# A 90-degree rotation of an 8192 x 8192 array: two early stores cut into halves with 8 KB reads

## The chip, the cores and the metric

The kernel runs on one core of one Trainium2 chip. The metric is the device time in microseconds; a kernel's time is the median of its runs. A profile is one execution taken by the hardware profiler, whose span is about 2 us shorter than the time of the run.

## The reference, cut to what matters

```python
def setup_inputs():
    return {"x": np.random.randn(8192, 8192).astype(np.float32), "k": 1}

def reference(x, k):
    return np.rot90(x, k)
```

The array is 268 MB. It has to be read once and written once.

## The kernel before

The array is worked through in macro tiles of 1024 rows by 4096 columns. A macro tile comes in by eight loads of 128 rows (2 MB each, one 16 KB run for each partition). VectorE copies each load, with blocks of columns mirrored, into eight chunk buffers; TensorE (PE in the profile) transposes 128 x 128 blocks into PSUM; ScalarE copies PSUM to an output tile and issues the store. A macro tile has eight outputs, numbered by `i`; each is stored by one transfer of 2 MB. `S` is the number of 128-row groups that one store carries: with `S = G = 4` each partition gives one run of 16 KB, with `S = PW = 2` a run of 8 KB.

```python
a_pool = ...(name="a_pool", bufs=2)     # loads
r_pool = ...(name="r_pool", bufs=63)    # chunks, 64 to a macro tile
o_pool = ...(name="o_pool", bufs=3)     # outputs
# ...
            for j in range(W // CH):
                ar = r_pool.tile([P, CH // P, P], dt, tag="ar")
                nc.vector.tensor_copy(out=ar[:], in_=a[:, j * CH : (j + 1) * CH]...[:, :, ::-1])
                chunks[t, j] = ar
# ... in store():
        for i, g0 in enumerate(range(0, W // P, G)):
            # ...
            S = PW if end and r0 + rows == N and g0 + G == W // P else G
            # ...
            for h in range(0, G, PW):
                # ... transpositions into ps[h // PW]
                nc.scalar.copy(o[:, G - PW - h : G - h, :], ps[h // PW])
                done = h + PW
                if done % S == 0:
                    # ...
                    nc.scalar.dma_start(out=dst, in_=o[:, G - done : G - done + S, :])
```

Of the kernel before, what the change touches and what calls it, by code (L numbers as in the profile page):

```python
# [2 lines left out]

# [5 lines left out]

P = 128  # L10




R = 1024
RT = R // P
LAST = [4, 4]
W = 4096
CH = 512
F = 4096  # L20
FP = 2048


def whole_reads(nc):






    for fn in nc.m.functions:
        for block in fn.blocks:
            for n, ins in enumerate(block.instructions):
                if not isinstance(ins, mybir.InstDMACopy):
                    continue
                src = ins.ins[0]
                ap = [list(d) for d in src.ap]
                if len(ap) == 3 and ap[2][0] == 1 and ap[1][0] == ap[2][1]:
                    ap = [ap[0], [1, 1], [1, ap[1][1] * ap[2][1]]]
                    block.instructions[n] = copy.replace(  # L40
                        ins,
                        ins=[copy.replace(src, ap=ap)],
                        ant_dge_precooked=False,
                    )


def macro_tiles(N, M):

    tiles = [(r0, RT, c0) for r0 in range(0, N, R) for c0 in range(0, M, W)]
    r0, _, c0 = tiles.pop()  # L50
    for n in LAST:
        tiles.append((r0, n, c0))
        r0 += n * P
    return tiles


@with_exitstack
def kernel(
    ctx: ExitStack,
    tc: tile.TileContext,  # L60
    x: bass.AP,
    k: bass.AP,
    out: bass.AP,
):
    nc = tc.nc
    assert k == 1, f"only k=1 supported, got {k}"
    nc.at_finalize(whole_reads)

    N, M = x.shape
    dt = x.dtype  # L70

    consts = ctx.enter_context(tc.tile_pool(name="consts", bufs=1))
    ident = consts.tile([P, P], dt)
    make_identity(nc, ident)

    a_pool = ctx.enter_context(tc.tile_pool(name="a_pool", bufs=2))
    r_pool = ctx.enter_context(tc.tile_pool(name="r_pool", bufs=63))
    o_pool = ctx.enter_context(tc.tile_pool(name="o_pool", bufs=3))
    psum_pool = ctx.enter_context(
        tc.tile_pool(name="psum", bufs=2, space=bass.MemoryType.PSUM)  # L80
    )

    loads = 0

    def load(r0, rt, c0):





        nonlocal loads
        chunks = {}
        for t in range(rt):


            if loads < RT and loads % 5 >= 2:
                a = o_pool.tile([P, W], dt, tag="o")
            else:
                a = a_pool.tile([P, W], dt, tag="a")
            loads += 1  # L100
            nc.sync.dma_start(  # L101
                out=a[:], in_=x[r0 + t * P : r0 + (t + 1) * P, c0 : c0 + W]
            )
            for j in range(W // CH):
                ar = r_pool.tile([P, CH // P, P], dt, tag="ar")
                nc.vector.tensor_copy(  # L106
                    out=ar[:],
                    in_=a[:, j * CH : (j + 1) * CH].rearrange(
                        "r (b m) -> r b m", m=P
                    )[:, :, ::-1],  # L110
                )
                chunks[t, j] = ar
            yield chunks

    def store(r0, rt, c0, chunks, end):





        rows = rt * P
        PW = 1
        while 2 * PW * rows <= FP:
            PW *= 2
        G = PW
        while 2 * G * rows <= F:
            G *= 2
        for i, g0 in enumerate(range(0, W // P, G)):
            if end and i % 2:
                ot = a_pool.tile([P, F], dt, tag="a")  # L130
            else:
                ot = o_pool.tile([P, F], dt, tag="o")
            o = ot[:, : G * rows].rearrange("m (g f) -> m g f", g=G)

            S = PW if end and r0 + rows == N and g0 + G == W // P else G


            ps = {}

            def transposes(t, ws):  # L140
                for w in ws:
                    g = g0 + w
                    nc.tensor.transpose(  # L143
                        ps[w // PW][:, PW - 1 - w % PW, t * P : (t + 1) * P],
                        chunks[t, g * P // CH][:, g % (CH // P), :],
                        ident,
                    )

            def psum_tile(h):
                pt = psum_pool.tile([P, FP], mybir.dt.float32, tag="ps")  # L150
                ps[h] = pt[:, : PW * rows].rearrange("m (g f) -> m g f", g=PW)

            if i == 0 and (rt == RT or r0 + rows < N):
                for h in range(G // PW):
                    psum_tile(h)
                for t in range(rt):
                    transposes(t, range(G))
            for h in range(0, G, PW):
                if h // PW not in ps:
                    psum_tile(h // PW)  # L160
                    for w in range(h, h + PW):
                        for t in range(rt):
                            transposes(t, [w])
# [4 lines that stand above are left out]
                    top = M - c0 - (g0 + done) * P  # L168
                    dst = out[top : top + S * P, r0 : r0 + rows].rearrange(
                        "(g m) f -> m g f", g=S  # L170
                    )
                    nc.scalar.dma_start(  # L172
                        out=dst, in_=o[:, G - done : G - done + S, :]
                    )
            yield

    tiles = macro_tiles(N, M)
    *most, before_last, last = tiles
    for m in most:
        *_, chunks = load(*m)  # L180
        for _ in store(*m, chunks, False):
            pass


    *_, chunks = load(*before_last)
    outputs = store(*before_last, chunks, True)
    rows = load(*last)
    for _ in range(last[1] - 1):
        next(rows)
    next(outputs)  # L190
    chunks = next(rows)
    for _ in outputs:
        pass
    for _ in store(*last, chunks, True):
        pass


# [1 line left out]
_INS = ['x', 'k']  # L199
_OUTS = [((8192, 8192), 'float32')]  # L200

_NUMBERS = {'k': 1}


# [26 lines left out]
```

## Time and profile before

| | before |
|---|---|
| time, median (6 runs) | 1267.82 us |
| bytes moved | 537.55 MB |
| usual DMA rate | 429 GB/s |
| first and last engine at the last store | 1258.41 and 1264.90 us |

The prediction below shows the main lines of this profile. Three more of the page matter later. Two are the queues of kind "instruction" (records, MB, share of the 16 engines); the third is the chain that ended last, by line.

```profile
q8 instruction: 32, 0.52, 0.2%
q14 instruction: 17, 0.14, 0.0%
...
DMA a<-in_x_dram 48%; DMA out_dram<-ot 30%; ACT ot L164 8%; DVE ar L106 8%; PE pt L143 5%; ACTq L172 0%; DVEq L106 0%; ACTq L164 0%; SPq L101 0%
```

### The profile page before, as it was taken

The page shows a single profiled execution, that of the slowest core. Times are in us where ns is not written, and L with a number is a line of the kernel's source. Part 1 is how long each engine was busy: PE and PEld are TensorE (multiplying, and loading weights), DVE is VectorE, ACT ScalarE, POOL GpSimd, SP SyncE. Part 2 cuts the span into 40 slices and gives each one's busy share as a digit, 9 for nine tenths or more (in the row PEclk, how much of TensorE's full clock was granted, in tenths as well). Part 3 has the DMA queues.
Part 4 walks back from the last instruction along what each step waited for, and adds up shares of the span by engine and source line. Part 5 has one row for each costly group of instructions (what it writes and reads, how often), then busy time and mean ns, then how long its engine had stood idle before and what let it go on. Part 6 is the DMA issues. An engine that isn't in the chain of part 4 may idle for free.

```text
span 1265.8 us, 10385 instructions
## 1 busy us (share of the span) xinstructions
PE 685.3 (54%) x4096; PEld 639.3 (51%) x4096; DVE 355.3 (28%) x1024; ACT 467.8 (37%) x257; POOL 0.7 (0%) x6
## 2 busy tenths in 40 slices
PE   1555545555555554564555546566464655546573
PEld 1544444554445454554545545565454655545572
DVE  4423322232222322232222322233222332223210
ACT  0433334333343333433424334243442434324363
POOL 0000000000000000000000000000000000000000
PEclk9977877768777777777777776776767776767777
DMA  9999999999999999999999999999999999999998
GB/s 398 426 429 429 428 429 429 428 431 427 429 429 429 428 430 429 429 428 429 429 429 428 429 421 430 427 430 429 423 429 428 418 429 428 428 429 425 428 422 334
DMA packets 37057, 537.55 MB, mean 425 GB/s; under 512 B 4112, under 2 KB 4112, under 8 KB 4112
## 3 DMA queue, kind: packets, MB, share of 16 engines
q10 hardware_dynamic: 18576, 268.44, 50.0%
q1 hardware_dynamic: 18432, 268.44, 49.8%
q8 instruction: 32, 0.52, 0.2%
q14 instruction: 17, 0.14, 0.0%
HBM read 268.44 MB, written 268.44 MB: 424 GB/s over the span
## 4 chain that ended last, share of the span: by engine, by line
DMA 77%; ACT 8%; DVE 8%; PE 5%; issue 1%; ACTq 0%; DVEq 0%; SPq 0%
DMA a<-in_x_dram 48%; DMA out_dram<-ot 30%; ACT ot L164 8%; DVE ar L106 8%; PE pt L143 5%; ACTq L172 0%; DVEq L106 0%; ACTq L164 0%; SPq L101 0%
## 5 line engine op out<-in xcount | busy, mean ns | idle before, releaser
L143 PE MATMUL pt<-ident,ar 128*128 128x128 f32 x4096 | 685.3, 344 | 560.7 <-ACT ot L164 396.1
L143 PEld LDWEIGHTS pt<-ident,ar 128*128 128x128 f32 x4096 | 639.3, 183 | 606.5 <-ACT ot L164 433.2
L164 ACT COPY ot<-pt 128x2048 f32<-128x2048 f32 x256 | 466.5, 1869 | 755.5 <-DMA out_dram<-ot 506.3
L106 DVE COPY ar<-a 128x512 f32<-128x512 f32 x1024 | 355.3, 422 | 865.4 <-DMA a<-in_x_dram 827.9
L164 ACT ACT_TABLE_LOAD x1 | 1.3, 1283 | 25.6 <-DVE ar L106 25.6
masks.py:199 POOL TENSOR_SCALAR_AFFINE_SELECT ident<-ident 128x128 f32<-128x128 f32 x1 | 0.3, 292 | 0.1
masks.py:197 POOL MEMSET ident<- 128x128 f32 x1 | 0.2, 204 | 0.3 <-POOLq L212 0.3
L212 POOL MEMSET const-bfloat16-1.0<- 128x1 bf16 x1 | 0.1, 102 | 0.0
L212 POOL MEMSET const-uint8-127<- 128x1 uint8 x1 | 0.1, 102 | 0.0
L212 POOL MEMSET const-float32-0.0<- 128x1 f32 x1 | 0.1, 99 | 0.2 <-issue 0.2
L212 POOL MEMSET const-float32-1.0<- 128x1 f32 x1 | 0.1, 99 | 0.0
## 6 DMA issues: line engine op xcount, KB each, us to landing
a<-in_x_dram SPq DMA_DIRECT2D x128, 2048.0 KB, 16.7
out_dram<-ot ACTq DMA_DIRECT2D x127, 2048.0 KB, 25.6
out_dram<-ot ACTq DMA_DIRECT2D x2, 1024.0 KB, 14.9
```

The source lines that it names most:

```text
L106: nc.vector.tensor_copy(out=ar[:], in_=a[:, j * CH : (j + 1) * CH].rearrange("r (b m) -> r b m", m=P)[:, :, ::-1],)
L143: nc.tensor.transpose(ps[w // PW][:, PW - 1 - w % PW, t * P : (t + 1) * P], chunks[t, g * P // CH][:, g % (CH // P), :], ident,)
L164: nc.scalar.copy(o[:, G - PW - h : G - h, :], ps[h // PW])
L212: nc = _bacc.Bacc("TRN2", target_bir_lowering=False, num_devices=1)
```

## The change

In the first macro tile, the fifth and the seventh output are stored in two halves, each with 8 KB reads. The intent, as I read it from the name `lead`, is to let the loads get ahead of the stores for a while. A record, below, is one run of bytes that a DMA engine moves, as the profile lists it; the lead is the bytes loaded minus the bytes stored so far. The prediction works out how half-sized store records could raise the lead.

```diff
-            S = PW if end and r0 + rows == N and g0 + G == W // P else G
+            lead = r0 == 0 and c0 == 0 and i in (4, 6)
+            S = PW if lead or (end and r0 + rows == N and g0 + G == W // P) else G
```

## The prediction

> **What bounds the kernel now.** I read first the share of each engine and the DMA rows, then the chain that ended last, then the waits, then the DMA throughput in short windows, and last the landing times of single transfers.
>
> The page of the kernel before, its busy shares, DMA rows, queues and chain:
>
> ```profile
> span 1265.8 us, 10385 instructions
> PE 685.3 (54%) x4096; PEld 639.3 (51%) x4096; DVE 355.3 (28%) x1024; ACT 467.8 (37%) x257; POOL 0.7 (0%) x6
> ...
> DMA  9999999999999999999999999999999999999998
> GB/s 398 426 429 429 428 429 429 428 431 427 429 429 429 428 430 429 429 428 429 429 429 428 429 421 430 427 430 429 423 429 428 418 429 428 428 429 425 428 422 334
> ...
> q10 hardware_dynamic: 18576, 268.44, 50.0%
> q1 hardware_dynamic: 18432, 268.44, 49.8%
> ...
> DMA 77%; ACT 8%; DVE 8%; PE 5%; issue 1%; ACTq 0%; DVEq 0%; SPq 0%
> ```
>
> No compute engine is over 54%; the 16 DMA engines are over 90% in every slice but the last. Loads (q1) and stores (q10) move the same bytes and take the same time. Where the chain names ACT, DVE or PE, the DMA share is still 9, so those links cost nothing. The waits agree: VectorE and ScalarE wait for transfers, and VectorE for a free chunk (a PE release) only six times.
>
> ```profile
> DVE ar L106 <- DMA a<-in_x_dram: 827.9, 123, 10.1
> ACT ot L164 <- DMA out_dram<-ot: 506.3, 91, 7.1
> ...
> DVE ar L106 <- PE pt L143: 37.5, 6, 7.6
> ```
>
> The floor follows: 537.55 MB at the usual 429 GB/s is 1253 us. The other 12.8 us of the span I look for in windows (columns after the engines: granted clock, DMA share, GB/s):
>
> ```profile
> 0.00:10.00 10.00, 1.08 (x4) 0.71 (x4) 1.86 (x6) 0.00 (x0) 0.70 (x6) 1.00 0.84 334
> ...
> 750.00:760.00 10.00, 7.25 (x58) 6.72 (x56) 2.77 (x8) 5.03 (x4) 0.00 (x0) 0.93 1.01 408
> 905.00:915.00 10.00, 8.86 (x64) 8.35 (x64) 2.87 (x9) 5.80 (x4) 0.00 (x0) 0.83 1.00 408
> 980.00:990.00 10.00, 6.30 (x29) 5.91 (x30) 2.77 (x8) 5.11 (x3) 0.00 (x0) 0.50 1.01 415
> 990.00:1000.00 10.00, 7.72 (x54) 7.25 (x54) 2.77 (x8) 5.89 (x4) 0.00 (x0) 0.84 0.99 405
> ...
> 1250.00:1260.00 10.00, 0.00 (x0) 0.00 (x0) 0.00 (x0) 0.00 (x0) 0.00 (x0) 0.50 0.89 369
> ```
>
> Three losses show. The head loses (429 - 334)/429 x 10 = 2.2 us. Four windows at the start of a macro tile's stores fall below 429: (21 + 21 + 14 + 24)/429 x 10 = 1.9 us, as a mean over the engines. The tail is uneven: of the last store's sixteen landings the first is at 1258.41 and the last at 1264.90, with a mean lag of 1.7 us, so the slowest DMA engine ends 4.8 us after the average. That skew grew over the run: 0.5 us at the first load, 1.7 us at the load landing at 105 us, 9.6 us at the stores near 1200 us. The steps that widen it early fall beside the small instruction-queue transfers (q8 and q14). The end is therefore the total work of the slowest of sixteen engines, which is never idle.
>
> **What the Trainium skill says.** "DMA: Bandwidth & Descriptors", section "Where 436 GB/s comes from", puts the ceiling at 435.2 GB/s for a core; the trace's 429 is 98.6% of it, so there is no bandwidth to win. The same page's section "Queues, rings and completion order" says that each engine round-robins between the queue rows with work, switching at packet boundaries. The trace agrees with equal turns: with 16 KB records on both sides the two queues share the rate evenly (about 214 GB/s each when I sum the records in 10 us steps from 100 us on). The same page, section "Why small descriptors are slow (HBM only)", gives a fixed overhead of about 3 cycles per packet, worst at 256 bytes; by that, 8 KB is far from the small case. The trace agrees: in the pure-store tail an 8 KB record takes 315 ns and a 16 KB one 626 ns (medians).
>
> **The change part by part.** A store of a full macro tile is 2 MB, 128 partitions of one 16 KB read each. The timeline of ScalarE shows the issues of the first macro tile: the fifth at 73.74 and the seventh at 93.41.
>
> ```profile
> 70.08 3.63 ACT L164 COPY ot<-pt 128x2048 f32<-128x2048 f32 x2 [6.71 <-DMA out_dram<-ot]
> 73.74 0.55 ACTq L172 DMA_DIRECT2D out_dram<-ot  x1
> ...
> 89.74 3.63 ACT L164 COPY ot<-pt 128x2048 f32<-128x2048 f32 x2 [6.30 <-DMA out_dram<-ot]
> 93.41 0.55 ACTq L172 DMA_DIRECT2D out_dram<-ot  x1
> ```
>
> - Added: two DMA issues of 0.55 us on ScalarE's queue. Each first half now goes out before the second copy, about 1.9 us earlier, and the second copy starts 0.6 us later. ScalarE stood idle 6.7 and 6.3 us ahead of these pairs, and two stores were still in flight (the fourth lands at 89.66), so this is worth 0 us.
> - Added: records. Per DMA engine, 2 stores x 8 partitions = 16 reads of 16 KB become 32 of 8 KB: 32 x 0.315 - 16 x 0.615 = +0.24 us at the durations seen beside loads, or 32 x 0.315 - 16 x 0.626 = +0.06 us against the tail's. Two more completion writes of 9 ns. Estimate +0.1 to +0.25 us, on every engine, so on the path.
> - Moved: bandwidth between the queues. With turns by record, loads get 16 KB for each 8 KB of a split store. Such a store takes 16 x (0.315 + 0.612) = 14.8 us rather than 9.8, and 16 load records, two loads' worth, pass meanwhile rather than 8. The fifth would land near 104, the seventh near 129, and the eighth near 138.7 instead of 128.5; loads would gain up to 2 loads or 4.2 MB on the stores. The bytes stay the same. I think this is the intent: to put the loads ahead.
> - What that lead could buy: loaded minus stored bytes, summed from the records, stand at 19.9 MB at 110 us and sink slowly to 18.7 MB at 1200 us. At the start of a later macro tile the fast engines run out of stores before the first output is ready: at 1142.80 the first engine had finished the old store, the next was issued at 1143.95. The slow windows of above fall there. A larger lead makes the first output ready earlier.
> - How much lead can stay: a row's copies need chunk buffers that PE frees. In the first macro tiles VectorE reaches a row some 10 us after the chunks it needs are free (estimate from the timelines of VectorE and PE), so loads can keep about one load, 2 MB, of the 4.2; beyond that VectorE waits for PE, loads pause, and stores take the full rate. DMA stays busy.
>
> Sum on the slowest engine: its landing interval is 9.76 us undisturbed and 9.9 to 10.2 in the slow windows, so these cost it about 0.8 us, not the mean's 1.9. Gain 0 to 0.8 us from there, cost 0.1 to 0.25 us for the records, and an open term: from about 360 us on, the slowest engine's interval is often 9.83 rather than 9.76, which I can't explain. Over some 95 intervals that is 6.5 us. If the new phase changes part of it, 1 to 3 us either way may follow. I take 1.3 us off in all: 0.7 for the slow windows, 0.15 back for the records, 0.75 as a share of the open term, chosen, not derived.
>
> **The rivals.**
> - Nothing but noise: the lead is lost again in the second macro tile to the buffer limit, and the end stays within 0.5 us of 1267.9. For it: the lead is bounded by 63 chunks and a slow drift; the end belongs to one engine. Against it: the drift of 1.1 MB in 1100 us is slow, so 2 MB should last.
> - A new wait: VectorE held by PE makes the load queue run dry while stores also pause at a macro tile's end. It would cost up to a few us, once per macro tile at worst: 1270 to 1275. Against it: two to three stores are queued at such times, and later stores only fill that gap better.
> - Loads before stores make the pure-store end longer. Pure stores run at 421 GB/s against 429; 2 MB more of it costs 0.1 us.
> - The skew itself falls or grows. If the slowest engine lost its 4.8 us the time would be 1263; nothing in the change moves the instruction transfers, so I give this little.
>
> **Range and chances.** The floor of 1253 us at 429 GB/s plus the launch makes 2% faster (1242.5) impossible. Slower by 2% is 25 us, more than two whole stores of idle DMA; no part offers it. The range holds the open term both ways. Predicted 1266.6 us, range 1263.0 to 1269.8; faster 0.005, within 2% 0.985, slower 0.01.
>
> **What would show it.** The store queue should have 288 more records (256 reads and 32 completion writes). The fifth and seventh outputs should drain in about 15 us, and loads landing between 90 and 130 us should come about 7.4 us apart instead of 9.76. VectorE's waits for PE should rise from 6. The windows under 420 GB/s between 700 and 1150 us should go, and the last store should still land over 4 us apart on its sixteen engines. If loads don't come faster there, turns go by something else than records and my step on sharing is wrong. If the slow windows go and the time stays, they were not on the slowest engine; if the time falls by over 4 us, the slowest engine's pace was what moved.

## The result, and the profile after

| | before | changed |
|---|---|---|
| time, median of 6 runs | 1267.82 us | 1267.49 us |
| lowest to highest | 1267.12 to 1267.90 | 1266.92 to 1267.88 |
| end of the last store in the profile | 1264.90 us | 1264.37 us |

The ratio is 0.9998, with a 95% interval from 0.9985 to 1.0011: the same.

The time stood still, but the inside of the run did not. The page of the changed kernel: DMA rate in 40 slices, the queues, and the chain by line.

```profile
GB/s 398 428 428 430 427 428 429 429 431 428 428 429 427 430 429 430 428 430 429 428 428 430 429 430 428 428 430 428 429 430 428 429 427 430 426 428 427 428 380 355
...
q10 hardware_dynamic: 18864, 268.44, 50.0%
q1 hardware_dynamic: 18432, 268.44, 49.7%
q8 instruction: 32, 0.52, 0.2%
q14 instruction: 17, 0.14, 0.0%
...
DMA out_dram<-ot 81%; ACT ot L167 13%; DMA a<-in_x_dram 3%; PE pt L146 0%; ACTq L175 0%; DVE ar L106 0%; ACTq L167 0%; SPq L101 0%
```

The store queue has the 288 more records predicted. The dips of 421, 423 and 418 GB/s in the middle slices are gone; in their place the 39th slice has 380 GB/s where before it had 422 (the 40th has 355 in place of 334). The chain that ended last now runs along stores (81%) rather than loads (3%): loads are ahead, as intended.

The windows of the changed kernel where the old one was slow, and those at the end of its loads:

```profile
750.00:760.00 10.00, 5.55 (x36) 5.31 (x35) 2.77 (x8) 3.64 (x2) 0.00 (x0) 0.83 1.01 431
905.00:915.00 10.00, 5.62 (x37) 5.38 (x37) 2.77 (x8) 3.64 (x2) 0.00 (x0) 0.84 1.01 429
980.00:990.00 10.00, 5.18 (x32) 4.95 (x32) 3.02 (x10) 3.77 (x3) 0.00 (x0) 0.83 1.01 431
990.00:1000.00 10.00, 5.37 (x32) 5.13 (x32) 3.02 (x10) 3.78 (x3) 0.00 (x0) 0.83 1.01 429
...
1210.00:1220.00 10.00, 7.26 (x39) 7.02 (x38) 2.77 (x8) 3.63 (x2) 0.00 (x0) 0.67 0.77 324
1220.00:1230.00 10.00, 9.21 (x82) 8.64 (x80) 0.00 (x0) 8.38 (x5) 0.00 (x0) 1.00 0.95 393
```

The same two late windows of the kernel before:

```profile
1210.00:1220.00 10.00, 6.30 (x35) 6.30 (x35) 2.96 (x10) 5.50 (x3) 0.00 (x0) 0.66 1.01 425
1220.00:1230.00 10.00, 8.61 (x75) 7.86 (x74) 0.72 (x3) 8.61 (x5) 0.00 (x0) 1.00 0.99 413
```

The reader sees a gain and its return. The four slow windows had lost 1.9 us of the mean engine's time; the two late windows now lose (101 + 20)/429 x 10 = 2.8 us more than before, and the DMA share of 0.77 says that engines stood idle there. Which engines idle? The landing times of single transfers tell it. A transfer lands in sixteen parts, one for each DMA engine. The lags of these parts behind the first, for a store near 1115 us and for the last store, worked out from the trace (us):

| | median engine, near 1115 us | third-last | second-last | last | second-last and last at the last store |
|---|---|---|---|---|---|
| before | 2.3 | 5.6 | 9.1 | 9.5 | 5.6, 6.5 |
| changed | 6.4 | 9.4 | 15.5 | 15.8 | 3.9, 4.0 |

In the changed kernel the fast engines run up to 15.8 us ahead of the two slowest, since loads leave them more to do. Then they wait. At the end of the loads, ScalarE's timeline shows why:

```profile
1205.64 3.63 ACT L167 COPY ot<-pt 128x2048 f32<-128x2048 f32 x2 [6.19 <-DMA out_dram<-ot]
1209.30 0.55 ACTq L175 DMA_DIRECT2D out_dram<-ot  x1
1214.80 3.63 ACT L167 COPY ot<-pt 128x2048 f32<-128x2048 f32 x2 [5.53 <-DMA out_dram<-ot]
1218.46 0.55 ACTq L175 DMA_DIRECT2D out_dram<-ot  x1
```

ScalarE waits for a store to land on all sixteen engines before it may fill that output buffer again ("<-DMA out_dram<-ot"). The store issued at 1209.30 had landed on the first engine at 1215.78; the next was issued at 1218.46, and the last load was over at 1214.13. So a fast engine had neither loads nor stores, while the slowest had work throughout. The two kernels' last stores end only 0.5 us apart.

The interval between the last landings of successive loads gives the pace of the slowest engine. In the changed kernel it is 9.77 us (median after 160 us), but for ten jumps to about 10.7 us, 108 to 128 us apart. Each jump from 280 us on comes 3 to 7 us after one of the 17 transfers of q14. That gave the theory for the experiments.

### The profile page after: what moved, and what is told of

Its sections match the earlier page's. It is cut to its first block, busy times and chain, and to the rows that moved or that the text cites. A ratio compares the mean times of both kernels' runs of the same rounds, so it can differ in the third digit from the quotient of the medians.

```text
span 1265.4 us, 10391 instructions
## 1 busy us (share of the span) xinstructions
PE 721.2 (57%) x4096; PEld 680.0 (54%) x4096; DVE 355.2 (28%) x1024; ACT 466.6 (37%) x257; POOL 0.7 (0%) x6
## 4 chain that ended last, share of the span: by engine, by line
DMA 84%; ACT 13%; issue 1%; PE 0%; ACTq 0%; DVE 0%; SPq 0%
DMA out_dram<-ot 81%; ACT ot L167 13%; DMA a<-in_x_dram 3%; PE pt L146 0%; ACTq L175 0%; DVE ar L106 0%; ACTq L167 0%; SPq L101 0%
## 5 line engine op out<-in xcount | busy, mean ns | idle before, releaser
L146 PE MATMUL pt<-ident,ar 128*128 128x128 f32 x4096 | 721.2, 357 | 526.2 <-ACT ot L167 470.2
L146 PEld LDWEIGHTS pt<-ident,ar 128*128 128x128 f32 x4096 | 680.0, 191 | 567.2 <-ACT ot L167 505.0
```

The costliest lines, as they stand in the source:

```text
L146: nc.tensor.transpose(ps[w // PW][:, PW - 1 - w % PW, t * P : (t + 1) * P], chunks[t, g * P // CH][:, g % (CH // P), :], ident,)
```

## The experiments

**Theory A:** the end is set by the slowest of sixteen DMA engines, and what makes it slow is that the refills of one compute engine's instructions (q14) all land on it; gains on the other engines become idle time. **Theory B:** the mean rate sets the end, and the new loss at 1210 to 1230 us merely happens to be as large as the old one. A second question is whether the lead comes from the record size.

### Same halves, but 16 KB reads

The two stores of the kernel before are cut by partitions instead.

```diff
+                    if r0 == 0 and c0 == 0 and i in (4, 6):
+                        for q in (0, P // 2):
+                            nc.scalar.dma_start(out=dst[q : q + P // 2],
+                                in_=o[q : q + P // 2, G - done : G - done + S, :])
+                        continue
```

> The kernel before, with the fifth and seventh store of the first macro tile in two halves too, but by partitions: two stores of 64 partitions whose reads stay 16 KB. If the loads' lead comes from the size of the record (turns between the queues go record by record), there is no gain here: loads land 9.76 us apart between 90 and 130 us, loaded minus stored bytes stay at 19.8 MB at 125 us, and the windows under 420 GB/s after 740 us stay. If the lead came from two transfers being queued in place of one, loads land 7.3 us apart as in the changed kernel, and the lead rises to 23 MB. Time within 1 us of 1267.8 either way.

Loaded minus stored bytes stood at 19.6 MB at 130 us against 22.4 to 23.1 in the changed kernel: no lead without the smaller record, so the number of transfers isn't it. The time missed the expectation: 1271.9 us median, 1268.4 to 1278.5, ratio 1.0034 [1.0012, 1.0055]. The windows of this kernel show two losses, one while the halves drain (first two lines) and one at the starts of later macro tiles:

```profile
90.00:100.00 10.00, 6.37 (x32) 6.13 (x32) 2.77 (x8) 3.64 (x2) 0.00 (x0) 0.66 1.00 400
110.00:120.00 10.00, 1.11 (x4) 0.71 (x4) 3.47 (x11) 1.53 (x1) 0.00 (x0) 0.57 1.00 401
...
910.00:920.00 10.00, 8.35 (x51) 7.70 (x49) 2.98 (x10) 7.34 (x4) 0.00 (x0) 0.65 0.97 359
990.00:1000.00 10.00, 8.26 (x55) 7.58 (x56) 3.00 (x10) 7.27 (x4) 0.00 (x0) 0.72 0.97 356
1150.00:1160.00 10.00, 8.46 (x55) 7.60 (x54) 2.99 (x10) 7.37 (x4) 0.00 (x0) 0.70 0.97 360
```

After the drain the lead was 19.1 MB, and it sank to 18.2 by 1190 us, where the kernel before still had 18.7. The windows are far deeper than those of before (405 to 415), and here the slowest engine is hit too: its intervals reach 11.2 us. So deep slow windows may cost; here they came with a longer run. I ran it again, together with a kernel that also gives the sixth and eighth store 8 KB reads (`lead` for `i in (5, 7)`).

> The store halves by partitions again, for their spread was 1268 to 1278 us. Reading so far: this kernel's lead of loads sinks to 18.0 MB, and at the starts of macro tiles its DMA rate falls to 350 to 400 GB/s, deep enough to lengthen the slowest engine's intervals to 11 us. If so it is slower again, by 2 to 6 us, with the same deep windows; if it was a disturbed chip, it is within 1 us of 1267.7.

> The same partition halves for the fifth and seventh store, and the sixth and eighth store in halves of 8 KB reads, to give the loads their lead back afterwards. If the low lead is what costs the partition halves their time, the lead is over 20 MB from 150 us on, the deep windows go, and the time falls to 1269 us or less (what is left is the loss while the halves themselves drain, up to 2 us). If the partition halves cost by themselves, it stays where the other run of this call is.

The halves alone: 1270.2 us median, but 1267.7 to 1281.8, ratio 1.0039 [1.0008, 1.0069], with the lead at 18.4 MB after the drain and windows below 400 GB/s. With the lead given back: 1268.4 us, 1268.2 to 1269.5, ratio 1.0007 [0.9996, 1.0019], the lead at 20.0 MB after the drain (19.2 at 1190 us) and no such windows later. Its drain still had windows near 390 and 403 GB/s, so the two kernels differ mostly in what came after. This supports that a low lead of loads is what costs time and spread, and that the change's record trick is a remedy for it. It does not show it: the two intervals overlap; from 800 us on the halves alone mostly had 18.6 to 19.1 MB, much like the kernel before (18.7 to 19.3), and still had a window near 400 GB/s; and why single runs of the halves differ by up to 14 us stays open.

### The opposite push

Two loads of the second macro tile are cut into 8 KB halves.

```diff
+            cuts = (0, W // 2, W) if r0 == 0 and c0 > 0 and t in (4, 6) else (0, W)
+            for u, v in zip(cuts, cuts[1:]):
+                nc.sync.dma_start(out=a[:, u:v], in_=x[r0 + t * P : r0 + (t + 1) * P, c0 + u : c0 + v])
```

> The kernel before, with two loads of the second macro tile (its fifth and seventh) in two halves of 8 KB each: the opposite push. The lead should fall from 19.8 MB by 1 MB or more, and the slow windows should come from 200 us on. Theory A, the end is the work of the slowest DMA engine, which is never idle: the time stays within 1 us of 1267.8, though the mean rate in the slow windows loses more than the 1.9 us of before. Theory B, the mean rate sets the end: the time rises by the extra loss of the windows, 1.5 us or more.

It took 1270.2 us, ratio 1.0018 [1.0006, 1.0030]. Turns by record were confirmed from the other side: the lead fell to 16.0 MB at 110 us. My expectation of lasting slow windows was wrong: the stores ran out altogether from 120 to 130 us, loads went on alone and the lead was back at 20.2 MB. That patch ran at 347 and then 385 GB/s, a loss of (82 + 44)/429 x 10 = 2.9 us of the mean engine's time, and the time rose by 2.6. The run does not decide between the theories: if all sixteen engines stood idle there, which I did not separate, theory A pays for it too.

### PE's instruction fetches (q8)

One kernel puts a small matmul ahead of every transposition, to double PE's instructions; the other replaces each pair of transpositions by one copying matmul, to halve them. Its output is wrong, which doesn't matter for the time.

```diff
+                    nc.tensor.matmul(ps[w // PW][:, PW - 1 - w % PW, t * P : t * P + 16], small, small[:, :16])
                     nc.tensor.transpose(
```

```diff
-                for w in ws:
-                    nc.tensor.transpose(ps[w // PW][...], chunks[...][:, g % (CH // P), :], ident)
+                for w in [w for w in ws if w % PW == 0]:
+                    nc.tensor.matmul(raw[w // PW][:, t * cols : (t + 1) * cols], small,
+                        src.bitcast(mybir.dt.bfloat16)[:, :, 1::2])
```

> The kernel before, with one small matmul (16 columns, overwritten at once by the transposition) ahead of each of the 4096 transpositions, so that PE's instructions double and their fetches (q8) go from 32 to 64 transfers of 16 KB. PE's busy time stays under 900 us. Theory A, the skew of the 16 DMA engines comes from the instruction fetches and the slowest engine sets the end: the time rises by 1.2 us (32 fetches of 0.62 us spread evenly over 16 engines) to 6 us (if they go mostly to few engines), and the last store's landings lie further apart than 6.5 us. Theory B, fetches do not matter: within 0.5 us of 1267.8.

> Wrong result on purpose: the kernel before with each pair of transpositions replaced by one bf16 matmul of 256 columns that copies, so that PE's instructions halve and its fetches go from 32 to 16. All transfers, copies and buffers as before. Theory A: the time falls by 0.6 us (16 fetches of 0.62 us, spread evenly) to 3 us (few engines), and the last store's landings come closer together than 6.5 us. Theory B: within 0.5 us of 1267.8.

The first told nothing on the question: PE became the bound, at 1378 us.

```profile
PE 1314.1 (95%) x8192; PEld 1054.0 (77%) x8192; DVE 364.1 (26%) x1025; ACT 477.8 (35%) x257; POOL 0.7 (0%) x6
```

My estimate of under 900 us of PE time was wrong; the added matmuls of 16 columns alone kept PE busy for 902.9 us, 221 ns each. The second took 1266.9 us against 1267.7, ratio 0.9995 [0.9984, 1.0007]: not clear of noise. By the interval, anything from 2.0 us faster to 0.9 us slower is possible, so the time decides nothing. The page has q8 at less than half:

```profile
q8 instruction: 15, 0.25, 0.1%
```

The landings say more. The last store's parts lie 4.9 us apart, closer than the 6.5 of before, as theory A expected. Near 1115 us the last engine is 7.8 us behind the first, but the second-last only 2.9 (15.8 and 15.5 in the changed kernel): one laggard of two is left. The one left is the one with jumps: ten of about 10.7 us, each some 6 us after a q14 transfer, and 9.76 us between. In the changed kernel the second-last engine has a smooth pace of 9.83 us (median after 360 us); here it has 9.76. So with half of PE's instructions the smooth laggard was gone, and the other one still set the end. Whether the fetches made it slow is not shown: the smooth pace is missing too in the second run of the partition halves (last and second-last engine: 9.77 and 9.76 us), where PE has all its instructions.

The same trace speaks on theory B. Seven windows of 10 us from 660 us on had 372 to 413 GB/s, a loss of 4.5 us of the mean where the kernel before lost 1.9; yet its profiled run, the slowest of its five, has a span only 1.1 us longer. So most of the 2.6 us did not reach the end.

### VectorE's refills (q14)

Each copy of 128x512 is cut into two of 128x256: nothing moves differently, but VectorE has 1024 more instructions.

```diff
-                nc.vector.tensor_copy(out=ar[:], in_=...)
+                half = CH // P // 2
+                for q in (0, half):
+                    nc.vector.tensor_copy(out=ar[:, q : q + half, :], in_=...[:, q : q + half, ::-1])
```

> MISLABELLED RUN, read as: the kernel BEFORE with each VectorE copy of 128x512 cut into two of 128x256, so VectorE has 2048 copies in place of 1024 (busy some 400 us of 1266); transfers, buffers and stores as before. In the trace of the changed kernel the last-landing DMA engine keeps 9.76 us per load but for nine jumps to 10.7, each 4 to 6 us after one 8 KB transfer of queue q14, some 118 us apart: about 128 VectorE instructions apart, so VectorE's instruction refills by my reading. Theory A (the slowest DMA engine carries VectorE's refills and sets the end): 17 q14 transfers become about 25, and the time rises by some 7 us (8 x 0.95) to 1275. Theory B (the mean rate in windows sets the end): 8 refills of 8 KB are nothing over 16 engines, and the time stays within 1 us of 1267.7.

> The changed kernel with the same doubling of VectorE's copies. Theory A: some 7 us up on the changed kernel, to about 1275, with about 17 jumps of 0.95 us in the last engine's landings, and no more slow windows than the changed kernel has. Theory B: within 1 us of 1267.5.

On the kernel before it took 1274.97 us (ratio 1.0060 [1.0047, 1.0073]), on the changed one 1274.47 (1.0052 [1.0040, 1.0065]), against 1267.77 for the kernel before in the same rounds. Theory A had said 1275. Of the jumps, which it expected to be about 17, the last landings of the second run show 11 over 10.3 us (16 in the first run). The page of the second run: VectorE has time to spare, its copies are twice as many, and q14 went from 17 to 25.

```profile
PE 729.2 (57%) x4096; PEld 692.3 (54%) x4096; DVE 430.6 (34%) x2048; ACT 466.5 (37%) x257; POOL 0.7 (0%) x6
...
q14 instruction: 25, 0.20, 0.0%
...
L108 DVE COPY ar<-a 128x256 f32<-128x256 f32 x2048 | 430.6, 287 | 790.9 <-DMA a<-in_x_dram 739.4
```

Eight more transfers of 8 KB, 66 KB in all, are worth 0.15 us at 429 GB/s, but the program is 7 us longer: 0.9 us for each. The lags near 1115 us name who pays: the last engine is 18.7 us behind the first and the second-last 9.9 us, where the changed kernel had 15.8 and 15.5. One engine alone got slower. Theory B is out for this cost. Why each transfer costs 0.9 us, where its own record lasts 0.31 us in the trace, no run shows.

Two more runs on the changed kernel looked at the others. ScalarE's copies were cut in two in the same way, and two of a load's eight VectorE copies were given to GpSimd.

```diff
-                nc.scalar.copy(o[:, G - PW - h : G - h, :], ps[h // PW])
+                for f in (0, rows // 2):
+                    nc.scalar.copy(o[:, G - PW - h : G - h, f : f + rows // 2], ps[h // PW][:, :, f : f + rows // 2])
```

> The changed kernel with each ScalarE copy of 128x2048 cut into two of 128x1024: 512 in place of 256, so two more q14 refills for ScalarE (256 instructions at 128 each). Theory A with one engine for each queue's refills: ScalarE's engine isn't the slowest, or is by little, so the time rises by 0 to 2 us. If all refills of q14 go to one engine, it rises by 1.9 us.

```diff
+                eng = nc.gpsimd if j % 4 == 3 else nc.vector
-                nc.vector.tensor_copy(
+                eng.tensor_copy(
```

> The changed kernel with two of a load's eight VectorE copies given to GpSimd, so that VectorE has 768 copies and two or three refills fewer. A try at a faster version. Theory A: 2 us down on the changed kernel, to about 1265.5, if the second-slowest engine follows (it lies within 0.1 us of the slowest at the last store); no gain if the second engine stays. A loss if GpSimd's copies are slow (over 4 us each) and hold the load buffers.

ScalarE doubled: q14 went from 17 to 19, and the time was 1267.89 us (ratio 1.0001), within the range expected. With GpSimd: VectorE had 768 copies, but q14 carried 18 transfers, one more and not fewer, and the time was 1268.14 us (1.0002), no gain. The landing intervals suggest why: the ten jumps went down to two, but the median interval of the last engine rose from 9.77 to 9.83 us. The last engine now seems to be another one, slow at a smooth pace, while the second-last has the jumps. I take it for the second of the two laggards: in the changed kernel the second-last had this pace, and in the kernel before, whose median interval is 9.82, it was mostly the last. The trace does not number the engines, so this is inferred from the landings.

### More of the change

All eight stores of the first macro tile in halves (`i >= 0` in place of `i in (4, 6)`).

> All eight stores of the first macro tile in halves of 8 KB reads. A lead asked for of eight loads, of which the 63 chunk buffers let one or so stay. If buffers cap it, loaded minus stored bytes peak near 23 MB and go back to 21 as in the changed kernel, and the time is within 1 us of the changed kernel's 1267.5. If more lead is worth more, the time falls below 1266.

The lead peaked at 23.5 MB and settled at 21.6, as the changed kernel settled at 21.1: this is what a cap by the buffers would give. The time was 1268.5 us, ratio 1.0004 [0.9991, 1.0016], so no gain is seen from more of it.

## Why the prediction was right or wrong

The time, 1267.49 us, lies in the range of 1263.0 to 1269.8, but the 1.3 us off that the prediction chose did not come: 0.33 us between the medians is within noise. That the middle was near is owed to the bound, which leaves little to win or lose; the two terms that were to bring the gain brought none. The prediction had named this outcome among its signs: "If the slow windows go and the time stays, they were not on the slowest engine."

- **What bounds the kernel** was right, and is the key: "the total work of the slowest of sixteen engines, which is never idle". Doubling VectorE's instructions supports it most, with 7 us for 66 KB on one engine. That the slowest is never idle was read from its even landing intervals, not seen by itself.
- **Turns by record** were right. In the changed kernel three of the four halves landed 7.3 us after what went before, and one 6.4, so 13.8 and 14.6 us for the two stores against the 14.8 predicted; four of the five loads between 94 and 127 us landed 7.3 to 7.9 us after the one before, where I had said 7.4. The fifth, seventh and eighth output landed at 104.1, 128.5 and 136.5 us (predicted 104, 129 and 138.7). That the lead would be capped was right too: it peaked at 23.1 MB and was 21.1 from 140 to 200 us, 1.4 MB over before; I had said about 2. It then sank, to 20.0 at 1190 us.
- **VectorE's waits for PE** rose from 6 to 23, as the step on buffers said. They cost nothing visible: the second line here stayed behind the wait for loads.

```profile
DVE ar L106 <- DMA a<-in_x_dram: 705.7, 106, 10.3
...
DVE ar L106 <- PE pt L146: 156.1, 23, 7.6
```

- **The slow windows** went, as predicted. The term "cost it about 0.8 us" on the slowest engine is the one mis-sized: the intervals of the last landings of loads after 160 us exceed 9.76 us by 9.4 us in sum before and by 9.5 us after. By this sum the slowest engine gained nothing from their going. The 1.9 us of the mean went to engines that were ahead and waited for it at 1210 to 1230 us. The step that failed is the reading that an interval of 9.9 to 10.2 us in a slow window was caused by the window. The one of 10.23 us that ends at 755 us comes 6.2 us after a q14 transfer, and so do those of 10.20 and 10.19 us that end at 627 and 863 us, where no window was slow.
- **The open term**, 0.75 us "chosen, not derived", brought nothing that can be seen. The pace of 9.83 us was not cured by the change: the second-last engine still has it. It seems to belong to a second slow engine, as the runs with GpSimd and with half of PE's instructions suggest.
- **The records' cost** of 0.1 to 0.25 us is too small to be seen in 0.33 us of difference between medians. The 0.315 us for 8 KB, said to be seen beside loads, came from the pure-store tail. Beside loads the changed kernel's trace has 0.309 us (median), so the sum would be 32 x 0.309 - 16 x 0.615 = 0.05 us: the cost was if anything nearer zero.
- **The rival** "nothing but noise" was right about the time. Of its reasons, the loss of the lead in the second macro tile did not happen (it was 1.3 MB over before at 1200 us); that "the end belongs to one engine" is what the runs support.
- **The tail** was told right in part: "the last store should still land over 4 us apart" measured 3.97.

What stays open: why the second laggard is slow by 0.07 us in each 9.76, and which DMA engine it is. The pace was gone in the run with half of PE's instructions, but also in the second run of the partition halves, so no run here separates its cause. That q14 carries instruction refills is inferred from its kind in the profile and from the counts (eight more for 1024 instructions on VectorE, two more for 256 on ScalarE); likewise q8 for PE (64 and 15 for 32).

## What to carry to other kernels

When all DMA engines are busy, look at the sixteen landing times of one transfer before trusting the mean rate: here a gain that did not reach the slowest engine came back as waiting at the end. In these runs record sizes set the shares of two queues, so a few smaller records let the loads lead; the one hint that this pays is the run where the lead had sunk. And in a kernel bound by DMA, count the instructions even of an engine with time to spare: here 1024 more on VectorE, busy for a third of the span, cost 7 us. Where two engines are nearly equally late, curing one alone shows no gain in the time, so look at both before calling a cause out.

## What the Trainium skill lacked or had wrong

- "DMA: Bandwidth & Descriptors", section "Queues, rings and completion order", names row 14 as runtime-internal with refills among its uses, but does not say that a compute engine's refills can weigh on one DMA engine; nor does "Runtime: NRT & Kernel Launch", section "Instruction fetch mechanics". Here 8 more transfers of 8 KB on q14, refills by my reading, made the program 7 us longer, 0.9 us for each.
- The same section says that turns between queues change at packets of several descriptors. Seen here: turns track the record in the profile. Where the trace lets one engine be followed (one record ends and a single one starts within some nanoseconds), a load record and a store record follow each other in 5027 of 5036 pairs of the changed kernel between 200 and 700 us, and in 202 of 206 in two stretches with 8 KB stores (96 to 104 and 122 to 128 us). The landing interval of 7.32 us alone would also fit turns of eight records.
- The same page, section "Rules for kernel authors", advises against splitting a transfer into partition halves since they serialize. The runs show a loss on top: 400 and 401 GB/s in place of 429 while such halves drained.
- The same page, section "Latency and other measured facts", has two of the sixteen DMA engines as usually slower in traces, with a guess tied to DMAs issued by GpSimd, and gives no size. Here SyncE and ScalarE issue all loads and stores, and two engines were still late: one with jumps of 0.95 us, one at 9.83 us for the 9.76 us of the others. Whether they are those two the trace does not tell.
